# The output projection of a hybrid attention block in seven products of quarter matrices instead of eight

## The chip, the core and the metric

The kernel runs on one core of one Trainium2 chip. The metric is the time of one execution on the device in microseconds (us), the median of several runs. A core has five engines with a queue each: TensorE (PE, its weight loads shown as PEld) multiplies matrices into PSUM, VectorE (DVE) and ScalarE (ACT) work elementwise from PSUM or SBUF, GpSimd (POOL) works elementwise from SBUF, and SyncE (SP) issues the DMA transfers. Each queue is worked off in order.

## What is computed

One layer with two attention branches. Cut to what matters here, with 1024 tokens and 1024 channels:

```
merged = sigmoid(mg_a) * (y_a @ w_branch_a) + sigmoid(mg_b) * (y_b @ w_branch_b)
x = x + gate * (merged @ w_out)
```

The last line is the output projection: a product of two 1024x1024 matrices in f32, then a row of gate factors and the residual.

## The kernel before

Every f32 matrix is kept as two parts, a high one rounded to the format of the fast matrix product (fp32r) and a low one, the rest. A product takes three matmuls, high with high, high with low and low with high (mm3, line 129). A matmul has 128 rows of K, 128 tokens and up to 512 columns.

The kernel has three stretches: normalization and the input projections, the attention of 16 heads with other matrix products woven in, and the output. The change begins behind the attention, at about 834 us.

**The merge.** fillers() (lines 957 to 1061) is a generator that emits the products that only have to be done in time. Its last 32 units multiply the branch outputs by w_branch, 16 for branch A and then 16 for branch B (kind 0 and 1; per block c of 128 channels two halves of 512 tokens, sh 0 and 1). A unit has 12 matmuls into one PSUM bank. For branch A, VectorE turns the bank into mA[c] (line 1036). For branch B it does three operations of 512 columns per unit: the gated product (mg, line 1039), the sum with mA (line 1040) and, one unit later, the low part hT_lo (line 1046); ScalarE writes the high part hT_hi between them (line 1041). hT_hi and hT_lo hold merged with channels on the partitions: block k of 8, 1024 tokens. The next block of branch weights is loaded by SyncE (load_w, line 102) and split by ScalarE (line 115) and VectorE (line 116). The banks go round over five (fbanks = "fgott").

**The weights w_out.** w_out_load(0) is emitted when branch A's products are (line 1058): four loads of 512 KB, in slots of U, a pool of 29 pieces of SBUF of 4 KB per partition which are handed out oldest first; a load waits on SyncE's queue until its slot's last reader is done, and all later transfers wait behind it. In branch B's units with c from 2 to 5 one piece each is split, the high part on ScalarE, the low part on GpSimd (line 1060). w_out_load(1) stands ahead of output().

**The output.** output() (line 1345) goes through 16 units, 8 tiles of 128 tokens for the left 512 columns and then for the right:

```
for k in range(KT):
    wh, wl = self.wo[c][k // 2]
    self.mm3(acc, self.hT_hi[:, k, sl], self.hT_lo[:, k, sl], wh[:, k % 2, ls], wl[:, k % 2, ls],
             k == 0, k == KT - 1)
nc.vector.tensor_tensor(out=ot[:, ls], in0=acc, in1=gbc[:, cs], op=ALU.mult)
nc.vector.tensor_tensor(out=ot[:, ls], in0=ot[:, ls], in1=x[:, ls], op=ALU.add)
nc.sync.dma_start(t["out"][st * P:(st + 1) * P, cs], ot[:, ls])
```

That is 24 matmuls and two VectorE operations (lines 1375 and 1376) per unit, in the banks t, t, o and f in turn. The last unit is done in two halves of 256 columns. GpSimd and ScalarE split the right half of w_out during the units 2 to 5. x comes in pieces of 512 columns from Hs, a pool of 11 slots of 2 KB.

Of the kernel before, what the change touches and what calls it, by code (L numbers as in the profile page):

```python
# [41 lines left out]
class Slots:  # L42
    """Equal pieces of SBUF, taken and given back by hand; the one given back longest ago goes first."""
# [31 lines left out]
class Net:  # L75
# [7 lines left out]
    # ------------------------------------------------------------ helpers  # L83
    def rsqrt(self, ssq, n, count, tag, between=iter(())):
        """between: other work of the vector engine, for the time each step waits for the one before."""
        nc, pool = self.nc, self.sp
        v, y, a = (pool.tile([P, 32], F32, tag=f"rs_{q}", name=f"{q}_{tag}", bufs=2)[:, 0:n] for q in "vya")
        nc.vector.tensor_scalar(out=v, in0=ssq, scalar1=1.0 / count, scalar2=EPS, op0=ALU.mult, op1=ALU.add)
        nc.vector.tensor_scalar(out=y.bitcast(I32), in0=v.bitcast(I32), scalar1=-0.5, scalar2=float(0x5F3759DF),
                                op0=ALU.mult, op1=ALU.add)  # L90
        for _ in range(3):
            next(between, None)
            nc.vector.scalar_tensor_tensor(out=a, in0=y, scalar=-0.5, in1=y, op0=ALU.mult, op1=ALU.mult)
            next(between, None)
# [143 lines left out]
    # ------------------------------------------------------------ phase 0  # L238
    def phase0(self):
# [71 lines left out]
        def broadcast_c():  # L311
            """c along the free dimension of every partition, through a diagonal and a product with ones."""
# [15 lines left out]
        def ada_rows(kt, bank):  # L328
            """The shift of a block whose rows lie on the partitions."""
# [193 lines left out]
    # ------------------------------------------------------------ latents  # L523
# [211 lines left out]
    # ------------------------------------------------------------ branch A operands  # L735
# [190 lines left out]
    def gate_sum(self, chs, engine="d"):  # L926
        """128 columns of the adaLN gate each."""
# [15 lines left out]
    def gate_row(self):  # L943
        """The gate as a row, quartered (the two factors of a half that the merge gates leave out)."""
# [12 lines left out]
    def fillers(self):  # L957
        """All GEMMs that only have to be done in time, some matmuls at a time; True where an accumulation ends."""
# [29 lines left out]
        low, mA = [], {}  # L988
        yield from self.g1b(first)
        for pos, (k, u) in enumerate(todo):  # L990
# [40 lines left out]
            else:  # L1031
# [5 lines left out]
                else:  # L1037
                    mf = mA[c][:, sl]
                    nc.vector.scalar_tensor_tensor(out=m, in0=m, scalar=1.0, in1=acc, op0=ALU.add, op1=ALU.mult)
                    nc.vector.tensor_tensor(out=mf, in0=mf, in1=m, op=ALU.add)  # L1040
                    nc.scalar.copy(self.hT_hi[:, c, sl], mf)
                    low.append((c, sh))
                    while len(low) > (pos + 1 < len(todo)):
                        c1, s1 = low.pop(0)
                        x = (slice(None), c1, slice(s1 * 512, s1 * 512 + 512))
                        nc.vector.tensor_tensor(out=self.hT_lo[x], in0=mA[c1][:, x[2]], in1=self.hT_hi[x].bitcast(F32),  # L1046
                                                op=ALU.subtract)
                        if s1:
                            U.put(mA.pop(c1))
                Hs.put(m)  # L1050
            if last:
# [3 lines left out]
                if kind == 0 and c == 7:  # L1055
                    for kk in range(4):
                        U.put(*self.y[kk])
                    self.w_out_load(0)
            if kind == 1 and sh == 1 and c in (2, 3, 4, 5):
                self.w_out_split(0, c - 2)  # L1060
            yield 1300. if kind == "t" and c < 8 else 1000.

    def w_out_load(self, c):
        self.wo[c] = [self.load_w(self.t["w_out"][c, k], [P, 2, 512], f"wo{c}{k}") for k in range(4)]

    def w_out_split(self, c, k):
        self.wo[c][k] = self.split(self.wo[c][k], f"wo{c}{k}", engine=self.nc.gpsimd)
# [63 lines left out]
    def prep_b(self, n):  # L1131
        """The same for heads n and n + 1 of branch B, turned together: rows 0-63 of a transpose are head n's."""
# [16 lines left out]
        def group(nm, src, vec, g):  # L1149
# [41 lines left out]
    def scores(self, n, i):  # L1191
        """Scores of q tile i of head n and their maximum; the rest of the softmax is returned."""
# [35 lines left out]
    def turn(self, n, g, j):  # L1228
        """Transposes k block j of P for q tiles 4g..4g+3; the products with V are returned."""
# [114 lines left out]
    # ------------------------------------------------------------ all  # L1344
    def output(self):
        nc, t, Hs, U = self.nc, self.t, self.Hs, self.U
        gbc = U.get([P, D], F32, "gbc")
        nc.sync.dma_start(gbc, self.gate_d.broadcast_to([P, D]))
        xt = {}

        def load(u):
            c, st = divmod(u, ST)
            xt[u] = Hs.get([P, 512], F32, f"xo{u}")
            nc.sync.dma_start(xt[u], t["x"][st * P:(st + 1) * P, c * 512:(c + 1) * 512])

        for u in range(3):
            load(u)
        for u in range(2 * ST):
            c, st = divmod(u, ST)
            if u + 3 < 2 * ST:  # L1360
                load(u + 3)
            if c == 0 and 2 <= st < 6:
                self.w_out_split(1, st - 2)
            sl = slice(st * P, (st + 1) * P)
            ot = Hs.get([P, 512], F32, f"ot{u}")
            x, n = xt.pop(u), 2 if u == 2 * ST - 1 else 1    # the last one in halves, for what follows its products
            for e in range(n):
                ls = slice(e * 512 // n, (e + 1) * 512 // n)
                cs = slice(c * 512 + ls.start, c * 512 + ls.stop)
                acc = self.bank("ttof"[(u + e) % 4], f"out{u}{e}")[:, ls]  # L1370
                for k in range(KT):
                    wh, wl = self.wo[c][k // 2]
                    self.mm3(acc, self.hT_hi[:, k, sl], self.hT_lo[:, k, sl], wh[:, k % 2, ls], wl[:, k % 2, ls],
                             k == 0, k == KT - 1)
                nc.vector.tensor_tensor(out=ot[:, ls], in0=acc, in1=gbc[:, cs], op=ALU.mult)
                nc.vector.tensor_tensor(out=ot[:, ls], in0=ot[:, ls], in1=x[:, ls], op=ALU.add)
                nc.sync.dma_start(t["out"][st * P:(st + 1) * P, cs], ot[:, ls])
            Hs.put(ot, x)

    def build(self):  # L1380
# [28 lines left out]
        self.passes, self.qk, self.v, self.p, self.gates, self.y, self.wo = {}, {}, {}, {}, {}, {}, {}  # L1409
        self.extra = []  # L1410
# [5 lines left out]
        with tc.manual_schedule():  # L1416
# [40 lines left out]
            self.w_out_load(1)  # L1457
# [3 lines left out]
# ---------------------------------------------------------------- host layout  # L1461
# [72 lines left out]
```

## Time and profile before

| what | us |
|---|---|
| median of 3 runs | 991.84 |
| lowest and highest run | 989.53 and 992.6 |
| profiled execution: its span (no other time of it is given) | 989.3 |

| engine | busy us | share of the span |
|---|---|---|
| PE | 954.5 | 96% |
| DVE | 659.8 | 67% |
| ACT | 475.7 | 48% |
| POOL | 250.8 | 25% |

A span runs from the first to the last instruction of an execution. Busy time is an average over all stages; what a stage is limited by shows in the slices of the page, in the order of time, and in what ended each engine's waits. A row of the timeline with x2 or more is several instructions in a row, with the time from the start of the first to the end of the last. The VectorE instructions overlap a little: the next can start before the one ahead is written off, so the distance between starts counts for a sum, not the duration.

### The profile page before, as it was taken

What the parts mean: (1) busy time and instruction counts of PE and PEld (TensorE: products, weight loads), DVE (VectorE), ACT (ScalarE), POOL (GpSimd) and SP (SyncE); (2) the same over time, 40 slices, a digit from 0 to 9 for tenths busy, and PEclk for the clock granted to TensorE, in tenths of its full rate; (3) what the DMA queues carried; (4) which work ended last, traced back from release to release, by engine and by line L of the source; (5) the groups of instructions that cost most, each with busy time, mean ns of one, the idle gap of its engine ahead of it and who ended that gap; (6) DMA issues with size and microseconds to landing.
All of it is one profiled execution on the core that took longest, in us unless ns stands there. A gap on an engine that the chain in (4) does not pass through costs nothing.

```text
span 989.3 us, 15335 instructions
## 1 busy us (share of the span) xinstructions
PE 954.5 (96%) x5550; PEld 833.1 (84%) x5550; DVE 659.8 (67%) x1399; ACT 475.7 (48%) x962; POOL 250.8 (25%) x279
## 2 busy tenths in 40 slices
PE   6479999999999999999999999999999999999998
PEld 6379999999998888888888888888888888887887
DVE  6997787676734766757667667677676767495222
ACT  6347653344334655655646566566565644143000
POOL 4843222220001222221223233333332220045000
PEclk9889999999999999999999999999999999999999
DMA  9733113346485223424224232231321554643321
GB/s 345 285 128 131 52 55 107 124 150 221 155 251 149 67 95 84 139 66 109 84 65 119 77 108 66 86 109 65 118 87 45 181 181 148 228 148 126 100 92 64
DMA packets 80700, 123.95 MB, mean 125 GB/s; under 512 B 5896, under 2 KB 47504, under 8 KB 80624
## 3 DMA queue, kind: packets, MB, share of 16 engines
q1 hardware_dynamic: 80624, 122.96, 38.1%
q8 instruction: 44, 0.72, 0.3%
q14 instruction: 32, 0.26, 0.1%
HBM read 87.29 MB, written 35.66 MB: 124 GB/s over the span
## 4 chain that ended last, share of the span: by engine, by line
PE 85%; DVE 8%; DMA 4%; issue 1%; ACT 1%; SPq 0%; POOL 0%; ACTq 0%; DVEq 0%; POOLq 0%
PE f L127 31%; PE b L127 12%; PE out L127 9%; PE s L127 8%; PE o L127 7%; PE pt L136 6%; PE q L127 3%; PE ckv L127 2%; PE kv L127 2%; DVE hT_lo L1046 1%; DVE hT_lo L365 1%; DMA ks_u<-ka_d 1%; DVE wada_u L339 1%; PE cq_s L127 1%; DVE xT L359 1%
## 5 line engine op out<-in xcount | busy, mean ns | idle before, releaser
L1240 ACT CAST pp_u<-pt 128x512 fp32r<-128x512 f32 x192 | 92.1, 480 | 181.6 <-PE pt L136 167.8
L1241 DVE TENSOR_TENSOR pp_u<-pt,pp_u 128x512 fp32r<-128x512 f32 x192 | 106.6, 556 | 79.2 <-ACT pp_u L1240 77.1
L127 PE MATMUL f<-hT_hi,hi_f_u 128*128 128x512 f32 x384 | 153.6, 400 | 0.0
L127 PE MATMUL f<-hT_hi,lo_f_u 128*128 128x512 f32 x384 | 153.4, 400 | 0.0
L127 PE MATMUL f<-hT_lo,hi_f_u 128*128 128x512 f32 x384 | 153.2, 399 | 0.0
L127 PE MATMUL s<-k_u,q_u 96*128 96x512 f32 (+6 forms) x480 | 116.4, 361 | 0.7 <-ACT p_h L1220 0.7
L127 PE MATMUL b<-hi_b_u,hT_hi 128*128 128x256 f32 x384 | 109.6, 285 | 0.0
L127 PE MATMUL b<-hi_b_u,hT_lo 128*128 128x256 f32 x384 | 108.6, 283 | 0.0
L127 PE MATMUL b<-lo_b_u,hT_hi 128*128 128x256 f32 x384 | 108.6, 283 | 0.0
L1224 POOL TENSOR_SCALAR p_u<-p_u,rs 128x640 f32<-128x640 f32 (+1 forms) x64 | 65.2, 1018 | 164.4 <-DVE rs L1223 95.9
L1224 POOL TENSOR_SCALAR p_h<-p_h,rs 128x128 f32<-128x128 f32 (+1 forms) x64 | 38.6, 603 | 245.5 <-DVE rs L1223 205.7
L1214 DVE TENSOR_REDUCE nm<-s 128x1 f32<-128x128 f32 (+7 forms) x128 | 97.0, 758 | 4.4
L127 PE MATMUL o<-pp_u,v_u 128*128 128x512 f32 (+7 forms) x384 | 94.2, 340 | 0.0
L127 PEld LDWEIGHTS f<-hT_hi,lo_f_u 128*128 128x128 f32 x384 | 72.4, 189 | 11.9
L127 PEld LDWEIGHTS f<-hT_lo,hi_f_u 128*128 128x128 f32 x384 | 72.5, 189 | 11.2
L127 PEld LDWEIGHTS f<-hT_hi,hi_f_u 128*128 128x128 f32 x384 | 72.5, 189 | 11.1
L127 PEld LDWEIGHTS s<-k_u,q_u 96*128 96x128 f32 (+2 forms) x480 | 76.7, 190 | 6.1 <-ACT p_h L1220 1.2
L127 PEld LDWEIGHTS o<-pp_u,v_u 128*128 128x128 f32 (+1 forms) x384 | 61.8, 161 | 19.6
L127 PEld LDWEIGHTS b<-lo_b_u,hT_hi 128*128 128x128 f32 x384 | 73.6, 192 | 0.3
L127 PEld LDWEIGHTS b<-hi_b_u,hT_hi 128*128 128x128 f32 x384 | 73.6, 192 | 0.3
L127 PEld LDWEIGHTS b<-hi_b_u,hT_lo 128*128 128x128 f32 x384 | 73.6, 192 | 0.0
L136 PEld LDWEIGHTS pt<-ident,p_u 128*128 128x128 f32 x416 | 52.7, 140 | 16.6
(319 smaller groups left out, 2072.0 us busy)
## 6 DMA issues: line engine op xcount, KB each, us to landing
raw_f_u<-in_w_t SPq DMA_DIRECT2D x24, 512.0 KB
wada_u<-in_w_ada SPq DMA_DIRECT2D x16, 512.0 KB
mg_d<-th_h SPq DMA_DIRECT2D x32, 256.0 KB
mg_h<-mg_d SPq DMA_DIRECT2D x32, 256.0 KB
raw_b_u<-in_w_b SPq DMA_DIRECT2D x12, 512.0 KB
x_u<-in_x SPq DMA_DIRECT2D x8, 512.0 KB
raw_wg_u<-in_w_gate SPq DMA_DIRECT2D x8, 512.0 KB
va_d<-vhl_u SPq DMA_DIRECT2D x8, 512.0 KB
```

The costliest lines, as they stand in the source:

```text
L127: self.nc.tensor.matmul(out, lhsT=l, rhs=r, start=start, stop=stop)
L136: self.nc.tensor.transpose(out=out, in_=in_, identity=self.ident)
L339: nc.vector.scalar_tensor_tensor(out=w, in0=w, scalar=1.0, in1=self.cb, op0=ALU.mult, op1=ALU.mult, accum_out=a)
L359: (nc.vector if engine == "d" else nc.gpsimd).tensor_scalar(out=xT[:, kt, c], in0=xT[:, kt, c], scalar1=gs[:, kt, 1:2], scalar2=gs[:, kt, ...
L365: nc.vector.tensor_tensor(out=lo[:, kt, c], in0=xT[:, kt, c], in1=hi[:, kt, c].bitcast(F32), op=ALU.subtract)
L1046: nc.vector.tensor_tensor(out=self.hT_lo[x], in0=mA[c1][:, x[2]], in1=self.hT_hi[x].bitcast(F32), op=ALU.subtract)
L1214: nc.vector.tensor_reduce(out=nm, in_=sv, axis=AX.X, op=ALU.max, negate=True)
L1224: nc.gpsimd.tensor_scalar(out=p[:, 0:w], in0=p[:, 0:w], scalar1=rs, scalar2=0.0, op0=ALU.mult, op1=ALU.add)
L1240: nc.scalar.copy(ph[:, c0:], pt[:, c0:])
L1241: nc.vector.tensor_tensor(out=pl[:, c0:], in0=pt[:, c0:], in1=ph[:, c0:].bitcast(F32), op=ALU.subtract)
```

## The change

The matrices merged and w_out are cut in quarters: A11 and A12 are the left and right 512 channels of tokens 0 to 511, A21 and A22 those of tokens 512 to 1023; B11, B12, B21 and B22 are the quarters of w_out. Seven products of sums of quarters take the place of the eight products of quarters (named by their weights in the code):

```
11: A11 B11    21: A12 B21    T3: (A11-A21)(B22-B12)
S1 = A21+A22   S2 = S1-A11    S4 = A12-S2
T1 = B12-B11   T2 = B22-T1    T4 = B21-T2
T2: S2 T2      T1: S1 T1      T4: A22 T4      22: S4 B22
```

Each product is four token tiles of 4 k blocks, 12 matmuls a unit of 512 columns, into four banks: "nsg" (s is one double bank, taken as two halves) and "ttof" in turn. Sums of the merged quarters, of the weights and of the results are tensor_tensor operations on VectorE, in place where they can be. hT holds A11 and A12 for tokens 0 to 511, and for 512 to 1023 A11-A21 in the blocks 0 to 3 and A22 in 4 to 7; S2, S1 and S4 are later written over A11, A11-A21 and A12. Quarters of w_out are loaded again where they are needed a second time. Cut to its core:

```diff
 # fillers()
+                    if sh and c < 4:
+                        mf = Hs.get([P, 512], F32, f"dA{c}")
+                        nc.vector.tensor_tensor(out=mf, in0=mA[c][:, 0:512], in1=mA[c][:, 512:1024], op=ALU.subtract)
                     nc.scalar.copy(self.hT_hi[:, c, sl], mf)
...
-                    self.w_out_load(0)
-            if kind == 1 and sh == 1 and c in (2, 3, 4, 5):
-                self.w_out_split(0, c - 2)
+                    self.wo_load(0, 0)
+            if kind == 1 and sh == 1 and c in (1, 2):
+                self.wo_split("11", self.wr[0, 0], (c - 1,), self.nc.gpsimd)
+            if kind == 1 and sh == 1 and c == 2:
+                U.put(*self.wr.pop((0, 0)))
+                self.wo_load(1, 1)
+                self.wo_load(0, 1)
+            if kind == 1 and sh == 1 and c == 6:
+                self.wo_sum((1, 1), (0, 1), ALU.subtract)
+                U.put(*self.wr.pop((0, 1)))
...
+    def wo_load(self, r, c):
+        self.wr[r, c] = [self.load_w(self.t["w_out"][c, 2 * r + i], [P, 2, 512], f"wo{r}{c}{i}") for i in range(2)]
+    def wo_sum(self, dst, other, op, into=0):
+        for i in range(2):
+            a, b = self.wr[dst][i], self.wr[other][i]
+            self.nc.vector.tensor_tensor(out=(a, b)[into], in0=a, in1=b, op=op)
+    def wo_split(self, name, raws, parts=(0, 1), engine=None):
+        engine = engine or nc.gpsimd
+        for i in parts:
+            hi, lo = (self.U.get([P, 2, 512], F32R, f"w{e}{name}{i}") for e in "hl")
+            for k in range(2):
+                nc.scalar.copy(hi[:, k], raws[i][:, k])
+                engine.tensor_tensor(out=lo[:, k], in0=raws[i][:, k], in1=hi[:, k].bitcast(F32), op=ALU.subtract)
 # output()
+        def sum_a(dst, a, b, op):
+            for k in range(4):
+                nc.vector.tensor_tensor(out=dst(k), in0=a(k), in1=b(k), op=op)
+        def split_a(src, k0, cols):
+            for k in range(4):
+                nc.scalar.copy(hi[:, k0 + k, cols], src(k))
+            for k in range(4):
+                nc.vector.tensor_tensor(out=lo[:, k0 + k, cols], in0=src(k), in1=hi[:, k0 + k, cols].bitcast(F32),
+                                        op=ALU.subtract)
+        def product(acc, k0, tok, name, ls=slice(0, 512)):
+            for k in range(4):
+                wh, wl = self.wo[name][k // 2]
+                sl = slice(tok * P, (tok + 1) * P)
+                self.mm3(acc[:, ls], hi[:, k0 + k, sl], lo[:, k0 + k, sl], wh[:, k % 2, ls], wl[:, k % 2, ls],
+                         k == 0, k == 3)
+        def finish(u, acc, add=None, ls=slice(0, 512), ready=None):
+            if add is not None:
+                nc.vector.tensor_tensor(out=ot[:, ls], in0=src, in1=add[:, ls], op=ALU.add)
+                src = ot[:, ls]
+            nc.vector.tensor_tensor(out=ot[:, ls], in0=src, in1=gbc[:, cs], op=ALU.mult)
+            nc.vector.tensor_tensor(out=ot[:, ls], in0=ot[:, ls], in1=x[:, ls], op=ALU.add)
+            nc.sync.dma_start(t["out"][st * P:(st + 1) * P, cs], ot[:, ls])
...
+        self.wo_load(1, 0)
+        self.wo_load(0, 0)
+        self.wo_split("T3", self.wr[1, 1], engine=nc.vector)
+        X = banks("nsg")
+        self.wo_split("21", self.wr[1, 0])
+        for i in range(4):
+            product(X[i], 0, i, "11")
+            nc.scalar.copy(s1[i], X[i])
+            if i == 0:
+                self.wo_sum((1, 1), (0, 0), ALU.add)
+            if i == 1:
+                sum_a(s1f, s1f, lambda k: mA[4 + k][:, R], ALU.add)
+            if i == 2:
+                sum_a(s2f, s1f, s2f, ALU.subtract)
+        self.wo_split("T2", self.wr[1, 1])
+        split_a(s2f, 0, L)
+        Z = banks("ttof")
+        for i in range(4):
+            product(Z[i], 0, 4 + i, "T3")
+            nc.vector.tensor_tensor(out=a7[i], in0=Z[i], in1=s1[i], op=ALU.add)
+            if i == 0:
+                sum_a(s4f, s4f, s2f, ALU.subtract)
+        self.wo_load(0, 1)
+        self.wo_load(0, 0)
+        split_a(s1f, 0, R)
+        X = banks("nsg")
+        for i in range(4):
+            product(X[i], 4, i, "21")
+            if i == 1:
+                self.wo_sum((1, 0), (1, 1), ALU.subtract)
+                self.wo_load(1, 1)
+            if i == 2:
+                self.wo_sum((0, 1), (0, 0), ALU.subtract)
+                self.wo_split("T1", self.wr[0, 1])
+            finish(i, X[i], s1[i])
+        self.wo_split("T4", self.wr[1, 0])
+        split_a(s4f, 4, L)
+        Z = banks("ttof")
+        for i in range(4):
+            product(Z[i], 0, i, "T2")
+            nc.vector.tensor_tensor(out=s1[i], in0=Z[i], in1=s1[i], op=ALU.add)
+            nc.vector.tensor_tensor(out=e[i], in0=Z[i], in1=a7[i], op=ALU.add)
+        self.wo_split("22", self.wr[1, 1])
+        X = banks("nsg")
+        for i in range(4):
+            product(X[i], 0, 4 + i, "T1")
+            nc.vector.tensor_tensor(out=s1[i], in0=X[i], in1=s1[i], op=ALU.add)
+            finish(4 + i, X[i], e[i])
+        Z = banks("ttof")
+        for i in range(4):
+            product(Z[i], 4, 4 + i, "T4")
+            finish(8 + i, Z[i], e[i])
+        X = banks("nsg")
+        for i in range(4):
+            n = 2 if i == 3 else 1
+            for h in range(n):
+                ls = slice(h * 512 // n, (h + 1) * 512 // n)
+                product(X[i], 4, i, "22", ls=ls)
+                finish(12 + i, X[i], s1[i], ls)
```

mA[0..7] now keep their slots until the output is under way, and the order of the output is tokens 0 to 511 left, 512 to 1023 right, 512 to 1023 left, 0 to 511 right.

## Rows read from the trace of the kernel before

**Rows 1.** The page: TensorE and VectorE in 40 equal slices of the span.
```profile
PE   6479999999999999999999999999999999999998
DVE  6997787676734766757667667677676767495222
```

**Rows 2.** Chain of waits that ended last: start us, length us, what.
```profile
895.64 0.61 DVE mg_h L1039
896.29 89.29 PE out L127 x408
986.06 0.43 DVE ot_h L1376
```

**Rows 3.** VectorE, timeline in the merge: start us, us, line, operation, [idle<-releaser].
```profile
853.74 0.69 DVE L1039 SCALAR_TENSOR_TENSOR mg_h<-mg_h,f 128x512 f32<-128x512 f32 x1 [2.03 <-PE f L127]
...
859.57 1.29 DVE L116 TENSOR_TENSOR lo_f_u<-raw_f_u,hi_f_u 128x512 fp32r<-128x512 f32 x2 [4.42 <-ACT hi_f_u L115]
860.78 0.68 DVE L1039 SCALAR_TENSOR_TENSOR mg_h<-mg_h,f 128x512 f32<-128x512 f32 x1
861.50 0.69 DVE L1040 TENSOR_TENSOR mA_u<-mA_u,mg_h 128x512 f32<-128x512 f32 x1
862.11 0.69 DVE L1046 TENSOR_TENSOR hT_lo<-mA_u,hT_hi 128x512 fp32r<-128x512 f32 x1
862.71 0.68 DVE L1039 SCALAR_TENSOR_TENSOR mg_h<-mg_h,f 128x512 f32<-128x512 f32 x1
...
898.80 1.46 DVE L1046 TENSOR_TENSOR hT_lo<-mA_u,hT_hi 128x512 fp32r<-128x512 f32 x2
```

**Rows 4.** Waits between 834 and 990: us in total, times, longest.
```profile
PE out L127 <- DVE mg_h L1039: 1.8, 1, 1.8
```

**Rows 5.** VectorE, timeline in the output.
```profile
903.69 0.69 DVE L1375 TENSOR_TENSOR ot_h<-out,gbc_u 128x512 f32<-128x512 f32 x1 [3.43 <-PE out L127]
904.42 1.32 DVE L1376 TENSOR_TENSOR ot_h<-ot_h,xo_h 128x512 f32<-128x512 f32 x1
909.13 0.69 DVE L1375 TENSOR_TENSOR ot_h<-out,gbc_u 128x512 f32<-128x512 f32 x1 [3.40 <-PE out L127]
...
982.72 0.42 DVE L1375 TENSOR_TENSOR ot_h<-out,gbc_u 128x256 f32<-128x256 f32 x1 [1.46 <-PE out L127]
983.18 0.43 DVE L1376 TENSOR_TENSOR ot_h<-ot_h,xo_h 128x256 f32<-128x256 f32 x1
```

**Rows 6.** VectorE, timeline around GpSimd's first pair of weight splits.
```profile
873.65 1.78 DVE L1046 TENSOR_TENSOR hT_lo<-mA_u,hT_hi 128x512 fp32r<-128x512 f32 x1
875.35 0.68 DVE L1039 SCALAR_TENSOR_TENSOR mg_h<-mg_h,f 128x512 f32<-128x512 f32 x1
876.06 1.07 DVE L1040 TENSOR_TENSOR mA_u<-mA_u,mg_h 128x512 f32<-128x512 f32 x1
```

**Rows 7.** GpSimd, timeline: the first pair of weight splits, and eight in a row.
```profile
873.06 3.52 POOL L116 TENSOR_TENSOR lo_wo_u<-raw_wo_u,hi_wo_u 128x512 fp32r<-128x512 f32 x2 [54.59 <-DVE mg_h L1039]
...
900.13 10.50 POOL L116 TENSOR_TENSOR lo_wo_u<-raw_wo_u,hi_wo_u 128x512 fp32r<-128x512 f32 x8 [5.65 <-ACT hi_wo_u L115]
```

**Rows 8.** SyncE's queue, timeline around 850.
```profile
844.78 7.29 SPq L102 DMA_DIRECT2D raw_wo_u<-in_w_out  x4
852.12 0.42 SPq L102 DMA_DIRECT2D raw_f_u<-in_w_br  x1
```

**Rows 9.** Chain of waits, around 855: the load that VectorE waits for.
```profile
852.12 6.73 DMA raw_f_u<-in_w_br
```

**Rows 10.** VectorE, timeline early in the kernel: 1024 columns.
```profile
72.57 1.23 DVE L365 TENSOR_TENSOR hT_lo<-xT,hT_hi 128x1024 fp32r<-128x1024 f32 x1
73.71 1.10 DVE L116 TENSOR_TENSOR lo_cq_u<-raw_cq_u,hi_cq_u 128x424 fp32r<-128x424 f32 x2
```

**Rows 11.** VectorE, timeline: two operations with a PSUM source in a row.
```profile
838.33 1.28 DVE L1036 SCALAR_TENSOR_TENSOR mA_u<-mg_h,f 128x512 f32<-128x512 f32 x2
```

**Rows 12.** ScalarE, timeline: eight copies of 512 columns in a row.
```profile
899.45 4.26 ACT L115 CAST hi_wo_u<-raw_wo_u 128x512 fp32r<-128x512 f32 x8
```

More of the change, by code (lines that the diff above doesn't have):

```diff
@@ L986, in first @@
                 load(0)
-        low, mA = [], {}
+        low, mA = [], self.mA
         yield from self.g1b(first)
@@ L1040, in fillers @@
                     nc.vector.tensor_tensor(out=mf, in0=mf, in1=m, op=ALU.add)
+                    if sh and c < 4:
+                        mf = Hs.get([P, 512], F32, f"dA{c}")
+                        nc.vector.tensor_tensor(out=mf, in0=mA[c][:, 0:512], in1=mA[c][:, 512:1024], op=ALU.subtract)
                     nc.scalar.copy(self.hT_hi[:, c, sl], mf)
-                    low.append((c, sh))
+                    low.append((c, sh, mf))
                     while len(low) > (pos + 1 < len(todo)):
-                        c1, s1 = low.pop(0)
+                        c1, s1, m1 = low.pop(0)
                         x = (slice(None), c1, slice(s1 * 512, s1 * 512 + 512))
[L1046 to L1049, printed above, removed]
+                        nc.vector.tensor_tensor(out=self.hT_lo[x], in0=m1, in1=self.hT_hi[x].bitcast(F32), op=ALU.subtract)
+                        if s1 and c1 < 4:
+                            Hs.put(m1)
                 Hs.put(m)
@@ L1057, in fillers @@
                         U.put(*self.y[kk])
-                    self.w_out_load(0)
-            if kind == 1 and sh == 1 and c in (2, 3, 4, 5):
-                self.w_out_split(0, c - 2)
-            yield 1300. if kind == "t" and c < 8 else 1000.
[L1063 to L1067, printed above, removed]
+                    self.wo_load(0, 0)
[8 more added lines that the diff above has]
+                U.put(*self.wr.pop((0, 1)))
+            yield 1300. if kind == "t" and c < 8 else 1000.
+    def wo_load(self, r, c):
[5 more added lines that the diff above has]
+    def wo_split(self, name, raws, parts=(0, 1), engine=None):
+        nc = self.nc
+        engine = engine or nc.gpsimd
[4 more added lines that the diff above has]
+                engine.tensor_tensor(out=lo[:, k], in0=raws[i][:, k], in1=hi[:, k].bitcast(F32), op=ALU.subtract)
+            self.wo.setdefault(name, []).append((hi, lo))
     def load_y(self, br, k):
@@ L1346, in output @@
         nc, t, Hs, U = self.nc, self.t, self.Hs, self.U
+        mA, hi, lo = self.mA, self.hT_hi, self.hT_lo
         gbc = U.get([P, D], F32, "gbc")
         nc.sync.dma_start(gbc, self.gate_d.broadcast_to([P, D]))
+        L, R = slice(0, 512), slice(512, 1024)
         xt = {}
+        order = [(st, 0) for st in range(4)] + [(st, 1) for st in range(4, 8)] + [(st, 0) for st in range(4, 8)] + \
+            [(st, 1) for st in range(4)]
         def load(u):
-            c, st = divmod(u, ST)
@@ L1353, in load @@
-            xt[u] = Hs.get([P, 512], F32, f"xo{u}")
-            nc.sync.dma_start(xt[u], t["x"][st * P:(st + 1) * P, c * 512:(c + 1) * 512])
-        for u in range(3):
-            load(u)
[L1358 to L1378, printed above, removed]
@@ new lines, in load, with four @@
+            if u < 16:
+                st, c = order[u]
+                xt[u] = Hs.get([P, 512], F32, f"xo{u}")
+                nc.sync.dma_start(xt[u], t["x"][st * P:(st + 1) * P, c * 512:(c + 1) * 512])
+        def four(name):
+            pair = [U.get([P, 2, 512], F32, f"{name}{i}") for i in range(2)]
+            return pair, [pair[i // 2][:, i % 2] for i in range(4)]
+        def sum_a(dst, a, b, op):
+            for k in range(4):
+                nc.vector.tensor_tensor(out=dst(k), in0=a(k), in1=b(k), op=op)
@@ new lines, in split_a, with banks @@
+        def split_a(src, k0, cols):
[4 more added lines that the diff above has]
+                                        op=ALU.subtract)
+        s1f = lambda k: mA[k][:, R]
+        s2f = lambda k: mA[k][:, L]
+        s4f = lambda k: mA[4 + k][:, L]
+        def banks(tags):
+            out = []
+            for tag in tags:
+                b = self.bank(tag, f"out_{tag}{len(out)}")
+                out += [b[:, 0:512], b[:, 512:1024]] if tag == "s" else [b]
+            return out
@@ new lines, in product @@
+        def product(acc, k0, tok, name, ls=slice(0, 512)):
[5 more added lines that the diff above has]
+        def finish(u, acc, add=None, ls=slice(0, 512), ready=None):
+            st, c = order[u]
+            x = xt[u]
+            cs = slice(c * 512 + ls.start, c * 512 + ls.stop)
+            ot = Hs.get([P, 512], F32, f"ot{u}{ls.start}")
+            src = acc[:, ls]
+            if add is not None:
[4 more added lines that the diff above has]
+            nc.sync.dma_start(t["out"][st * P:(st + 1) * P, cs], ot[:, ls])
+            Hs.put(ot)
+            if ls.stop == 512:
+                Hs.put(xt.pop(u))
+                load(u + 4)
@@ new lines, in done @@
+        def done(name):
+            for pair in self.wo.pop(name):
+                U.put(*pair)
+        for u in range(4):
+            load(u)
+        self.wo_load(1, 0)
+        self.wo_load(0, 0)
+        self.wo_split("T3", self.wr[1, 1], engine=nc.vector)
+        X = banks("nsg")
+        s1s, s1 = four("p1_")
+        self.wo_split("21", self.wr[1, 0])
[4 more added lines that the diff above has]
+                self.wo_sum((1, 1), (0, 0), ALU.add)
+                U.put(*self.wr.pop((0, 0)))
+            if i == 1:
+                sum_a(s1f, s1f, lambda k: mA[4 + k][:, R], ALU.add)
+            if i == 2:
+                sum_a(s2f, s1f, s2f, ALU.subtract)
@@ new lines, in output @@
+        done("11")
+        self.wo_split("T2", self.wr[1, 1])
+        split_a(s2f, 0, L)
+        Z = banks("ttof")
+        a7s, a7 = four("a7_")
+        for i in range(4):
[3 more added lines that the diff above has]
+                sum_a(s4f, s4f, s2f, ALU.subtract)
+        done("T3")
+        self.wo_load(0, 1)
+        self.wo_load(0, 0)
+        split_a(s1f, 0, R)
+        for k in range(4):
+            U.put(mA.pop(k))
@@ new lines, in output @@
+        X = banks("nsg")
[3 more added lines that the diff above has]
+                self.wo_sum((1, 0), (1, 1), ALU.subtract)
+                U.put(*self.wr.pop((1, 1)))
+                self.wo_load(1, 1)
+            if i == 2:
+                self.wo_sum((0, 1), (0, 0), ALU.subtract)
+                U.put(*self.wr.pop((0, 0)))
+                self.wo_split("T1", self.wr[0, 1])
+                U.put(*self.wr.pop((0, 1)))
+            finish(i, X[i], s1[i])
@@ new lines, in output @@
+        done("21")
+        self.wo_split("T4", self.wr[1, 0])
+        split_a(s4f, 4, L)
+        for k in range(4, 8):
+            U.put(mA.pop(k))
+        Z = banks("ttof")
+        es, e = four("e_")
+        for i in range(4):
+            product(Z[i], 0, i, "T2")
+            nc.vector.tensor_tensor(out=s1[i], in0=Z[i], in1=s1[i], op=ALU.add)
+            nc.vector.tensor_tensor(out=e[i], in0=Z[i], in1=a7[i], op=ALU.add)
+        done("T2")
+        U.put(*self.wr.pop((1, 0)))
+        self.wo_split("22", self.wr[1, 1])
@@ L1409, in build @@
         self.passes, self.qk, self.v, self.p, self.gates, self.y, self.wo = {}, {}, {}, {}, {}, {}, {}
+        self.mA, self.wr = {}, {}
         self.extra = []
@@ L1456, in build @@
                 self.U.put(*self.y[kk])
-            self.w_out_load(1)
             self.output()
```

## The prediction

> **What bounds the kernel now.** I read the slices of the page first, then the chain of waits, then VectorE's timeline at the end, then GpSimd's and SyncE's. The slices show TensorE at nine tenths or more from the fourth slice on, and VectorE, once the start is over, at nine tenths only in slice 36; its last four are 5, 2, 2, 2 [rows 1]. One slice is 24.7 us, so the output has an idle VectorE and a full TensorE. The chain agrees: its last long piece is 89.3 us of output matmuls, with one VectorE operation behind it that starts at 986.06 and lasts 0.43 [rows 2]. But the chain reaches these matmuls through VectorE, not through TensorE: at the hand-over from merge to output TensorE waited 1.8 us for VectorE [rows 4], and the first output unit took 903.69 - 896.29 = 7.40 us where the next took 909.13 - 903.69 = 5.44 [rows 2, 5], 1.96 more, since VectorE still wrote low parts until 898.80 + 1.46 = 900.26 [rows 3]. That lag began when VectorE sat idle 4.4 us for a load of branch weights [rows 3], which took 6.73 us from its issue [rows 9]; SyncE had put four loads of w_out ahead of it, issued between 844.78 and 852.07 [rows 8].
>
> I count time t from the end of TensorE's merge work. Its first unit of branch B ended at 853.74 [rows 3]; a unit of 12 matmuls is half of 5.44, 2.72 us; 15 more end at 894.5. So the output's matmuls could have begun at t = 0 and began at t = 1.8; VectorE's last operation ended at 986.49, t = 92.0.
>
> **TensorE's side.** Before: 15 units of 24 matmuls, two halves of 2.87 us (the first ends at 982.72, 5.44 x 14 + 2.87 behind 903.69). After: 27 units of 2.72 and two halves of 1.43, together 76.3 us. The first product reads only blocks 0 to 3 of tokens 0 to 511, written long before, and the free banks n and s, so the 1.8 us and the 1.96 us go too. TensorE alone would end at t = 76.3 instead of 985.58 - 894.5 = 91.1, 14.8 us earlier; one more VectorE operation behind the last half costs 0.4. By TensorE alone the gain were 14.3 us.
>
> **VectorE's side.** The edits give VectorE nearly all that they take from TensorE. Distances between starts are the price. Two SBUF inputs of 512 columns: 0.61 (862.11 - 861.50) [rows 3]. 1024 columns: 73.71 - 72.57 = 1.14 [rows 10]. One PSUM source with an independent operation next: two in 1.28 us, so 0.60 each [rows 11]. An operation that reads the result of the one ahead starts 0.73 behind it (904.42 - 903.69) [rows 5]. In the output:
> 28 operations of 512 columns from SBUF (the T3 split, S1, S2, S4 and three splits, 4 each): 17.1;
> three sums of weights, 2 operations of 1024 each: 6.8;
> 16 with a PSUM source (4 behind T3, 8 behind T2, 4 behind T1): 9.6;
> 15 finishes of a chain of three, 0.73 + 0.73 + 0.61 = 2.07: 31.0;
> the last one in halves, 0.46 (983.18 - 982.72 [rows 5]) + 0.46 + 0.43 twice: 2.7.
> Sum 67.2 us, against 16 x 2 operations before.
>
> [...] My rows make PSUM and SBUF sources alike [rows 3, 11]. [...]
>
> *The hand-over.* Only two loads of w_out instead of four now stand ahead of the branch weights. I take half of the 6.73 us as gone [rows 9], so VectorE resumes at about 856.3 instead of 859.57, and its split is done at 857.5. From there: 15 units of 862.71 - 860.78 = 1.93 [rows 3], 29.0; four new subtractions for A11-A21, each reading what was just written, 0.73, 2.9; two more splits of branch weights at 1.21, 2.4; the new sum of weights 2 x 1.14, 2.3; the last low part 0.8; and four GpSimd operations in place of eight. A pair of those lengthens VectorE by 1.09 and 0.38 (1.78 and 1.07 for 0.69) [rows 6], 0.74 per GpSimd operation, 3.0. VectorE ends at 897.8, t = 3.3. Bounds: 2.6, where it is no later than TensorE's last unit, and 6.6, where the load comes no earlier. TensorE does not wait, since five banks go round.
>
> *GpSimd beside VectorE.* An operation of GpSimd and one of VectorE with two SBUF inputs do not overlap [rows 6, 7]: GpSimd's pair took 3.52 us, two pauses of 0.6 and two of 1.15 alone (eight in a row took 10.50, with two VectorE operations between); VectorE's operation from 873.65 took 1.78, one such 1.15 longer, while the one with a PSUM source beside it at 875.35 took its plain 0.68. They take turns. Now GpSimd splits five quarters behind the merge, 4 operations each. Walking the queues: the splits 21 and T2 fall on VectorE's sums and on S1 and S2, so 8 x 1.15 = 9.2; T1's fall on two finishes, whose first operation reads PSUM and goes past: 3.1; T4's fall on the low parts of S4, 4 x 1.15 = 4.6; 22's fall on the eight PSUM operations of product T2, nothing. Sum 16.9. Bounds: 12 of them at the 0.63 that the operation at 904.42 lost [rows 5], 7.6; all 20 at 1.16, 23.2. I take the walk, nearest to the rows of a busy VectorE.
>
> *The sum.* 3.3 + 67.2 + 16.9 = 87.4. In this walk VectorE never waits for TensorE: it starts 3.3 late, enters product 21 some 10 us behind, and ends 9 behind TensorE's last matmul. So the end is VectorE's: t = 87.4 against 92.0, **4.6 us less**, a span of 984.7 for 989.3. The page gives no time outside the span; the median of the runs is 2.5 above it, and 4.6 off 991.84 gives 987.2.
>
> **Waits checked.** T3's weights need four ScalarE copies at 0.53 [rows 12] and four subtractions behind t = 3.3: ready near 6, wanted at 10.9. 21's are ready near 14, wanted at 21.8. T2's and S2's near 25, wanted at 32.6. The quarters for T1 are loaded into slots that product T3 reads until t = 21.8; even with 6.73 us [rows 9] they land by 29 and VectorE asks for them at 39. T1's own split is the late one: its sum ends near 41, its last low part near 47, wanted from 43.5 on. TensorE stalls about 2 us there, which a 9 us slack swallows. SyncE's queue: the new loads stand ahead of the stores, and the second load of B11 waits for a slot that VectorE's sum frees, near 893, landing near t = 4, wanted near 6. The banks of one set are free 2 us before TensorE returns to them in product T2, the tightest place.
>
> **Rivals.** (a) *TensorE stays the bound.* GpSimd's operations cost VectorE about 0.63 each or less, and the sum falls to 3.3 + 67.2 + 7.6 = 78.1, where TensorE's 76.3 + 2 + 1.4 decide with 79.7: 12.3 less, 979.5. For it: VectorE idled 3.4 us in each output unit [rows 5]. Against it: the 1.78 us [rows 6]. Between it and the forecast lie 8 to 10 us of gain.
> (b) *Slower: the two halves of bank s count as one tile.* If a product into the second half has to wait until VectorE has read the first, then in products 21, T1 and 22 the third unit stands behind VectorE's finish of the second. Product 21 ends near 43 instead of 32.6, T1 near 69, T4 near 80, and in 22 the wait comes again: the last half ends near 92, VectorE at 93.4: 1.4 us slower than before, 993.2, and as much more as VectorE is late. It decides where that finish lies behind TensorE's own unit, from product 21 on. No row shows two halves of a bank in use by two engines.
> (c) *The hand-over stays late.* The load comes no earlier, or all 20 GpSimd operations cost their full 1.16: 6.6 or 23.2 in place of one term gives t = 90.7 or 93.7, 1.3 less to 1.7 more; 990.5 to 993.5.
>
> **How the numbers follow.** Forecast 0.53, rival (a) 0.17, (b) 0.12, (c) 0.18. The likeliest gives 987.2, its own range 984 to 991. A measurement of this kernel can tell about 0.3% from no change, 3 us. Faster by more: three quarters of the forecast, 0.40, and (a), together 0.57. Slower by more: the tails of (b) and (c) with further delay, 0.10. Within: 0.33. The range from 980.5 to 994.0 leaves out most of (a)'s far end and the tail where (b) or (c) meet more delay, some 2 in 10.
>
> **What would show it.** Right: no wait of TensorE at the hand-over; output matmuls of 76 to 79 us with one stall at T1's first unit; VectorE at nine tenths or more to the end, ending 7 to 11 us behind the last matmul; VectorE operations of 1.7 us beside GpSimd's in products 11 and T3. Wrong: VectorE waiting for TensorE in the last two products (then (a)), TensorE waiting before the third unit of a product in n, s, g (b), or VectorE's last low part of the merge beyond 900 (c). A stall that VectorE's queue spends on a DMA would overturn the walk.

## The result, and the profile after

The changed kernel takes 998.91 us, median of 14 runs, beside 989.96 us for 14 runs of the kernel before on the same chips: ratio 1.0084, 95% interval 1.0067 to 1.0100, **slower by 0.84%**. The forecast was 987.2 us, faster. The profiled run took 998.97 us.

The first thing to look at is the page, whose slices are now 24.9 us long.

```profile
span 997.2 us, 15352 instructions
...
PE 950.0 (95%) x5490; PEld 827.4 (83%) x5490; DVE 721.4 (72%) x1472; ACT 491.3 (49%) x990; POOL 264.7 (27%) x287
...
PE   6579999999999999999999999999999999998887
...
DVE  5997887686734666757657677667677766799986
...
PEclk9889999999999999999999999999999999999899
```

TensorE's last four slices, 9, 9, 9, 8 before [rows 1], are 8, 8, 8, 7, and VectorE's are 9, 9, 8, 6 for 5, 2, 2, 2. Neither engine is full to the end: two engines that take turns look like this. Who waits for whom is read from the waits of the kernel after, from 834 us to the end (engine, tile, line, releaser: us in total, times, longest). These are all the waits of TensorE for a reader of the output's banks, and the two longest of VectorE for TensorE there.

```profile
DVE ot_h L1428 <- PE out_s L127: 4.1, 3, 1.9
DVE p_u L1506 <- PE out_s L127: 3.2, 1, 3.2
PE out_g L127 <- DVE ot_h L1428: 1.1, 1, 1.1
PE out_s L127 <- ACT p_u L1452: 4.0, 1, 4.0
PE out_s L127 <- DVE ot_h L1428: 9.2, 3, 4.7
```

The wait of 1.8 us at the hand-over [rows 4] is gone, as forecast. In its place TensorE waits five times, 14.3 us in all, and each time for a reader of a bank of the set n, s, g (X in the code): four times of the double bank s, once of g. VectorE waits for TensorE in return. TensorE's timeline says where in a product that happens (start, duration, instruction, and in brackets the idle time ahead with its releaser). The rows are the first matmul of the output, of the unit that runs straight on into s, of each unit that waited, and of the units that follow the first two waits.

```profile
894.96 0.39 PE L127 MATMUL out_n<-wh_u,hT_hi 128*128 128x512 f32 x1
...
897.68 0.39 PE L127 MATMUL out_s<-wh_u,hT_hi 128*128 128x512 f32 x1
...
904.52 0.80 PE L127 MATMUL out_s<-wh_u,hT_hi 128*128 128x512 f32 x1 [3.95 <-ACT p_u L1452]
...
908.87 0.40 PE L127 MATMUL out_g<-wh_u,hT_hi 128*128 128x512 f32 x1
...
932.77 0.79 PE L127 MATMUL out_s<-wh_u,hT_hi 128*128 128x512 f32 x1 [4.69 <-DVE ot_h L1428]
...
938.06 0.59 PE L127 MATMUL out_g<-wh_u,hT_hi 128*128 128x512 f32 x1
...
961.24 0.50 PE L127 MATMUL out_s<-whT_u,hT_hi 128*128 128x512 f32 x1 [3.75 <-DVE ot_h L1428]
...
985.70 0.50 PE L127 MATMUL out_s<-wh_u,hT_hi 128*128 128x512 f32 x1 [0.79 <-DVE ot_h L1428]
...
991.32 0.39 PE L127 MATMUL out_g<-wh_u,hT_hi 128*128 128x256 f32 x1 [1.14 <-DVE ot_h L1428]
```

It is always the same place: the first unit into s runs straight on (897.68), the second unit into s, the third of its product, waits until the first unit into s has been read. That holds for products 11, 21, T1 and 22. The last wait is the second half of the last unit, which lies in the same bank g as the first half; before, the two halves had banks of their own.

The waits are not all of it. The unit behind the wait of 4.69 us took 938.06 - 932.77 = 5.29 us, the one behind the wait of 3.95 us took 908.87 - 904.52 = 4.35, where a unit takes 2.72 elsewhere. The windows of 5 us show the reason (us, then busy time and count of PE, PEld, DVE, ACT, POOL, then PEclk, DMA share, GB/s).

```profile
900.00:905.00 5.00, 1.05 (x4) 0.62 (x3) 5.00 (x6) 4.44 (x9) 3.06 (x2) 0.94 0.00 0
905.00:910.00 5.00, 5.00 (x17) 3.92 (x17) 5.00 (x3) 0.59 (x1) 4.61 (x3) 0.72 0.00 0
910.00:915.00 5.00, 5.00 (x23) 4.13 (x22) 4.88 (x7) 3.20 (x7) 1.96 (x2) 1.00 0.00 0
...
935.00:940.00 5.00, 5.00 (x16) 3.90 (x15) 3.11 (x4) 4.45 (x9) 3.90 (x3) 0.65 0.45 163
```

From 905 to 910 TensorE is busy all the time and gets through 17 matmuls where 23 fit into the next 5 us: the mean granted clock is 0.72, for 1.00 in the next 5 us; from 904.5 to 906 alone it is 0.50. TensorE had stood idle for 3.95 us ahead of it.

**The sum of it.** TensorE's output began at 894.96 and ended at 991.32 + 1.71 = 993.03, 98.1 us where the forecast had 76.3. By products, from one first matmul to the next: 11 took 16.6 us instead of 10.9, 21 took 18.5, T1 16.6, and 22 took 13.7 where its three units and two halves were to take 11.0. That is 5.8 + 7.6 + 5.7 + 2.7 = 21.8 us, all in the four products that use n, s and g; T3, T2 and T4 in the four single banks took their 10.9. Of it 14.3 are the waits above and some 6.5 the slower units behind them; the rest is the last matmul ahead of each wait, which runs out its 0.39 us where the next one otherwise starts 0.23 behind it.

### The profile page after: what moved, and what is told of

Its sections match the earlier page's. It is cut to its first block, busy times and chain, and to the rows that moved or that the text cites. A ratio compares the mean times of both kernels' runs of the same rounds, so it can differ in the third digit from the quotient of the medians.

```text
span 997.2 us, 15352 instructions
## 1 busy us (share of the span) xinstructions
PE 950.0 (95%) x5490; PEld 827.4 (83%) x5490; DVE 721.4 (72%) x1472; ACT 491.3 (49%) x990; POOL 264.7 (27%) x287
## 4 chain that ended last, share of the span: by engine, by line
PE 57%; DVE 8%; issue 2%; ACT 1%; DVEq 0%; ACTq 0%
PE f L127 31%; PE s L127 8%; PE o L127 7%; PE pt L136 6%; PE out_s L127 2%; DVE hT_lo L1400 1%; DVE hT_lo L1049 1%; DVE mg_h L1039 1%; PE out_g L127 1%; DVE mA_u L1040 1%; PE kt L136 1%; DVE ot_h L1428 1%; PE qt L136 1%; PE out_t L127 1%; DVE ot_h L1430 1%
## 5 line engine op out<-in xcount | busy, mean ns | idle before, releaser
L136 PEld LDWEIGHTS pt<-ident,p_u 128*128 128x128 f32 x416 | 52.7, 140 | 16.6
```

What stands on the lines that cost most here:

```text
L136: self.nc.tensor.transpose(out=out, in_=in_, identity=self.ident)
```

## The experiments

**1 and 2: the banks, from both sides.** Four banks that are four tiles in place of n, s, s, g:

```diff
-                b = self.bank(tag, f"out_{tag}{len(out)}")
-                out += [b[:, 0:512], b[:, 512:1024]] if tag == "s" else [b]
+                out += [self.bank(tag, f"out_{tag}{len(out)}")]
...
-        X = banks("nsg")
+        X = banks("wxyz")
...
+            self.ps2 = ctx.enter_context(tc.tile_pool(name="ps2c", bufs=1, space=PSUM))
```

> The changed kernel with four single banks in place of n, the two halves of s, and g; nothing else is different. Theory (the two halves of bank s count as one tile for the queue): TensorE's four waits before the third unit of a product (4.0, 4.7, 3.3 and 0.3 us in the changed kernel's profile) and the half-clock stretches behind them go, TensorE's output takes about 78 us, VectorE sets the end near 88 us after the merge's last matmul as in the prediction's walk, the span is 984 to 988 and the ratio to before 0.994 to 0.999. Rival (TensorE waits because VectorE and ScalarE are late with what the product reads, whatever the bank): the waits stay at other units, span 994 or more, ratio 1.004 or more.

Measured: 990.01 us beside 990.86, ratio 0.9992 (0.9980 to 1.0004): as fast as before, and 8.9 us less than the change as it is. The waits in the expected text are given as 3.3 and 0.3 us for T1 and 22; the rows above have 3.75 and 0.79. The waits went as the theory said, but the span, 989.0 us, lies just above its range of 984 to 988; where the difference went stands in the next part. The waits of TensorE in the output that are left, from the waits of this kernel:

```profile
PE out_z L127 <- DVE ot_h L1427: 8.0, 1, 8.0
...
PE out_w L127 <- POOL wlT_u L1089: 1.4, 2, 0.7
```

No third unit waits any more. The 1.4 us are the late split of T1, forecast at about 2. The 8.0 us stand ahead of the second half of the last unit, in the same bank and tile z as the first. VectorE's timeline of this kernel has its last operation of the merge, and its end:

```profile
900.10 1.46 DVE L1049 TENSOR_TENSOR hT_lo<-mA_u,hT_hi 128x512 fp32r<-128x512 f32 x2
...
984.82 0.42 DVE L1427 TENSOR_TENSOR ot_h<-out_z,p_u 128x256 f32<-128x256 f32 x1 [2.10 <-PE out_z L127]
...
985.74 0.42 DVE L1430 TENSOR_TENSOR ot_h<-ot_h,xo_h 128x256 f32<-128x256 f32 x1
```

From 901.56 to 986.16 are 84.6 us, with one wait of 2.1: the last half has to be computed after VectorE asks for it, and behind 8 idle us it took 2.94 us, at a granted clock of 0.50, where the half ahead of it took 1.59 (the clock of that stretch is in the last row here, from the windows of this kernel).

```profile
945.00:970.00 25.00, 25.00 (x112) 20.65 (x111) 24.62 (x33) 1.42 (x3) 11.63 (x8) 1.00 0.35 103
...
980.00:985.00 5.00, 2.93 (x12) 2.63 (x12) 2.76 (x7) 0.00 (x0) 0.00 (x0) 0.50 0.36 131
```

The other side: the kernel before, with its units put alternately into the two halves of one double bank.

```diff
+        sd = self.bank("s", "outs")
...
-                acc = self.bank("ttof"[(u + e) % 4], f"out{u}{e}")[:, ls]
+                acc = (sd[:, 0:512], sd[:, 512:1024])[(u + e) % 2][:, ls]
```

> The kernel before, but the output's units alternate between the two halves of the double bank s instead of t, t, o, f. Theory: each unit waits until VectorE has read the unit before, at least 0.75 us for each of 16 boundaries, more where the clock is granted lower behind the wait: 12 to 30 us longer than before, span 1001 to 1020. Rival (halves are told apart by address): a half is read 0.7 us after its unit and needed again 5.4 us later, so the span stays at 989 to 991.

Measured: 1005.4 us, one run. VectorE is far from full here (it waits 76.1 us for TensorE), and still every unit waits, 16 times and 12.4 us in all; from TensorE's timeline of this kernel:

```profile
901.26 0.50 PE L127 MATMUL outs<-hi_wo_u,hT_hi 128*128 128x512 f32 x1 [0.79 <-DVE ot_h L1376]
...
907.78 0.50 PE L127 MATMUL outs<-hi_wo_u,hT_hi 128*128 128x512 f32 x1 [0.78 <-DVE ot_h L1376]
```

A unit starts every 907.78 - 901.26 = 6.52 us, not 5.44: 0.78 of waiting for VectorE's read of the other half, one operation, 0.16 in which the last matmul ahead of the wait runs out, and 0.14 of slower matmuls behind it. The half that a unit writes to was read a whole unit earlier; what it waits for is the read of the other one, which has just been filled. So the coupling is a property of the double tile, not of a late VectorE; a late VectorE only makes the wait longer.

**3 to 5: is VectorE's side as priced?** In experiment 3, on top of 1, ScalarE copies in the place of GpSimd's twenty subtractions (the low parts of five weight quarters are left out):

```diff
-                engine.tensor_tensor(out=lo[:, k], in0=raws[i][:, k], in1=hi[:, k].bitcast(F32), op=ALU.subtract)
+                if engine is nc.vector or name == "11":
+                    engine.tensor_tensor(out=lo[:, k], in0=raws[i][:, k], in1=hi[:, k].bitcast(F32), op=ALU.subtract)
+                else:
+                    nc.scalar.copy(lo[:, k], raws[i][:, k])
```

> Four single banks as in e1, and the low parts of the weights of products 21, T2, T1, T4 and 22 are copies made by ScalarE, so that GpSimd does nothing in the output. What is left out: the subtraction in these low parts. Theory (GpSimd's operations hold VectorE's up, 16.9 us by the walk): VectorE falls from 88 to about 73 us and TensorE's 76 to 79 us decide: span 974 to 979. Rival (GpSimd costs VectorE little, VectorE's own work is the bound): within 3 us of e1.

Measured: 982.72 us, one run. VectorE's timeline of this kernel:

```profile
902.11 1.47 DVE L1049 TENSOR_TENSOR hT_lo<-mA_u,hT_hi 128x512 fp32r<-128x512 f32 x2
...
977.47 0.42 DVE L1433 TENSOR_TENSOR ot_h<-ot_h,xo_h 128x256 f32<-128x256 f32 x1
```

and its waits between 900 us and the end:

```profile
DVE hT_lo L1403 <- ACT hT_hi L1401: 6.6, 2, 3.8
...
DVE ot_h L1430 <- PE out_z L127: 0.9, 1, 0.9
```

977.89 - 903.58 = 74.3 us, of which 7.5 are waits, 6.6 of them for ScalarE, which now has twenty more copies. The span, 980.7, lies 1.7 above the theory's range. TensorE's first and last matmul of the output, and its only wait between them, show that this is not the output's doing:

```profile
898.31 0.39 PE L127 MATMUL out_w<-wh_u,hT_hi 128*128 128x512 f32 x1
...
974.83 0.39 PE L127 MATMUL out_z<-wh_u,hT_hi 128*128 128x256 f32 x1 [1.48 <-DVE ot_h L1430]
...
976.24 0.28 PE L127 MATMUL out_z<-wh_u,hT_lo 128*128 128x256 f32 x1
```

From 898.31 to 976.52 are 78.2 us, within the theory's 76 to 79; but the output began 3.8 us later than the 894.5 from which the theory counted. VectorE's waits for ScalarE fell in time that it had to spare: TensorE waited for VectorE once, 1.48 us, where the same wait is 1.14 in the change as it is. VectorE's own work is 74.3 - 7.5 = 66.8 us; the forecast's sum was 67.2. With GpSimd beside it (experiment 1) it was 84.6 - 2.1 = 82.5, so GpSimd's twenty operations cost VectorE 15.7 us, 0.79 each, where doing them itself would cost 0.61; forecast 16.9.

In experiment 4, also on top of 1, VectorE does the low parts of 21, T2, T1 and T4 itself; those of 22 stay with GpSimd.

```diff
-        self.wo_split("21", self.wr[1, 0])
+        self.wo_split("21", self.wr[1, 0], engine=nc.vector)
...
```

> Four single banks as in e1, and the low parts for products 21, T2, T1 and T4 are made by VectorE instead of GpSimd (22 stays on GpSimd). Theory: 16 operations more on VectorE cost 16 x 0.61 = 9.8 us and about 1 us of waiting for ScalarE's copies, the 16.9 us lost beside GpSimd go: 6 us less than e1, span 978 to 983, ratio 0.988 to 0.993. [...]

Measured: 986.81 us, ratio 0.9964 (0.9946 to 0.9983): faster than before, by less than expected (span 984.9 for 978 to 983). VectorE's timeline of this kernel shows what was left out of account:

```profile
939.45 4.68 DVE L1089 TENSOR_TENSOR wlT_u<-raw_wo_u,whT_u 128x512 fp32r<-128x512 f32 x4
944.06 3.58 DVE L1400 TENSOR_TENSOR hT_lo<-mA_u,hT_hi 128x512 fp32r<-128x512 f32 x4
```

Four such subtractions take 2.49 us elsewhere. GpSimd's four for 22, which in experiment 1 ran from 951.12 to 956.63 beside operations with a PSUM source, 0.67 or 0.68 us each, now begin at 938.95 and 945.47 and meet these: 2.2 + 1.1 = 3.3 us. The wait ahead of the last half is there too, 7.3 us.

Experiment 5 takes both away: 22 goes to VectorE as well, and the last unit is not divided.

```diff
-        self.wo_split("22", self.wr[1, 1])
+        self.wo_split("22", self.wr[1, 1], engine=nc.vector)
...
-            n = 2 if i == 3 else 1
+            n = 1
```

> As e4, with 22's low parts on VectorE too and the last unit undivided. Theory (VectorE alone sets the end, and a half in the bank that VectorE still reads costs a wait of TensorE): in e4 the last half began 3 us late and cost 2.7 us more than one chain of three would; 22's four GpSimd operations lengthened VectorE by 3.4 us where four of its own cost 2.4. So 3.7 us less than e4: ratio to before 0.990 to 0.995, span near 981. Rival (the tail is a matter of the last transfer's size): twice the bytes at the end eat the gain, ratio 0.996 as e4.

Measured: 983.75 us beside 990.68, **ratio 0.9926 (0.9908 to 0.9945)**, as the theory had it: this version beats both kernels. The two edits were made together, so what each gives alone is not shown. The windows of this kernel, from 905 to 970 us:

```profile
905.00:970.00 65.00, 65.00 (x288) 53.87 (x287) 64.25 (x99) 17.95 (x33) 0.00 (x0) 1.00 0.40 128
```

and VectorE's last operation, from its timeline:

```profile
979.22 0.69 DVE L1430 TENSOR_TENSOR ot_h<-ot_h,xo_h 128x512 f32<-128x512 f32 x1
```

TensorE is busy for 65 us on end at a granted clock of 1.00 and done at about 973; VectorE follows and ends at 979.9. Both engines are full: what the change was to look like. By the terms above VectorE needs 66.8 + 20 x 0.61 - 0.6 for the undivided last unit = 78.4 us; from 901.8 to 979.9 are 78.1.

**6 and 7: two half measures in the change as it is.** In experiment 6 the two halves of s are not neighbours in a product: n, s, g, s.

```diff
-            return out
+            return [out[0], out[1], out[3], out[2]] if len(tags) == 3 else out
```

> The changed kernel with the order n, first half of s, g, second half of s, so that a unit lies between the two halves. Theory (a product into one half waits for the reader of the other): the waits of 4.0, 4.7 and 3.3 us move from the third unit to the fourth, and each is shorter by up to one unit, 2.7 us: span 988 to 994. Rival (the third unit waits for what it reads): the waits stay at the third unit, span 996 to 999.

Measured: 992.84 us, one run: 6.1 us less than the change as it is, about two thirds of what experiment 1 gave back. The wait has moved to the fourth unit; from TensorE's timeline of this kernel:

```profile
906.28 0.50 PE L127 MATMUL out_s<-wh_u,hT_hi 128*128 128x512 f32 x1 [1.49 <-ACT p_u L1452]
...
934.56 0.80 PE L127 MATMUL out_s<-wh_u,hT_hi 128*128 128x512 f32 x1 [6.19 <-DVE ot_h L1428]
```

Product 11's wait fell from 3.95 to 1.49. T1's fell from 3.75 to 1.52, and 22's is gone but for the 1.14 between the two halves of the last unit. That of 21 grew from 4.69 to 6.19: TensorE came to it earlier, VectorE no earlier.

Experiment 7 leaves the double bank and gives VectorE the low parts of 21, T2, T1 and T4, as experiment 4 did.

> The changed kernel with the two halves of s as they are, and the low parts for 21, T2, T1 and T4 on VectorE. Theory (the waits are as long as VectorE is behind TensorE): VectorE gains 6 us by the end of product T2, so the waits in products 21 and T1 shrink by most of their 4.7 and 3.3 us with the half-clock stretches behind them, the one in product 11, which waits for ScalarE, stays: span 987 to 992. Rival (the waits do not depend on VectorE's lag): span 996 to 999.

Measured: 996.2 us, one run: 2.7 us less than the change as it is. The span, 994.4, lies between the range of the theory and that of the rival. From TensorE's timeline of this kernel, the third units of 11, 21 and T1:

```profile
905.21 0.80 PE L127 MATMUL out_s<-wh_u,hT_hi 128*128 128x512 f32 x1 [3.96 <-ACT p_u L1452]
...
931.49 0.50 PE L127 MATMUL out_s<-wh_u,hT_hi 128*128 128x512 f32 x1 [2.68 <-DVE ot_h L1428]
...
958.46 0.50 PE L127 MATMUL out_s<-whT_u,hT_hi 128*128 128x512 f32 x1 [3.27 <-DVE ot_h L1428]
```

The wait for ScalarE (3.96) stays, as expected. That of 21 shrank from 4.69 to 2.68, so the waits do depend on how late VectorE is. T1's is still 3.27, for 3.75, and VectorE's timeline ahead of T1 shows why:

```profile
941.59 4.67 DVE L1089 TENSOR_TENSOR wlT_u<-raw_wo_u,whT_u 128x512 fp32r<-128x512 f32 x4
946.19 3.58 DVE L1400 TENSOR_TENSOR hT_lo<-mA_u,hT_hi 128x512 fp32r<-128x512 f32 x4
```

As in experiment 4, GpSimd's four operations for 22 meet these subtractions, and VectorE loses 2.2 + 1.1 = 3.3 us, about as much as T1 then waits.

## Why the prediction was wrong

**The step that failed** is the one on the free banks, in "Waits checked": "The banks of one set are free 2 us before TensorE returns to them in product T2, the tightest place". It looked at the return to a set from the next product but one, and "TensorE's side" took n, s and g for four banks that are free one by one. The two halves of s are one tile, and in these runs a unit into one half stood until the other had been read: experiment 1 takes the double tile away and the waits go, experiment 2 puts one into the kernel before and they come. With that, TensorE's term of 76.3 us became 98.1, and the walk in which "VectorE never waits for TensorE" became one in which each waits for the other. The sign that was set for (b), TensorE waiting before the third unit of a product in n, s, g, is what the trace shows. Rival (b) had named this mechanism, its place in 21, T1 and 22, and the sign, at a chance of 0.12; its evidence was put as "no row shows two halves of a bank in use by two engines", which left open what experiment 2 settles.

**Rival (b)'s price was too small as well**, 1.4 us slower than before for 7.9 by the spans. By its own walk, counted from the end of the merge's matmuls (894.96 here), 21 was to end at 43, T1 at 69, T4 at 80 and VectorE at 93.4; they ended at 46.0, 73.5, 84.4 and 99.4. Three things were missing:
- Product 11. Its results are read by ScalarE, not by VectorE, so (b) passed it over. ScalarE's copy of the second unit stood behind eight weight casts; from ScalarE's timeline of the kernel after:

```profile
899.11 2.18 ACT L1088 CAST whT_u<-raw_wo_u 128x512 fp32r<-128x512 f32 x4
901.20 2.17 ACT L1088 CAST wh_u<-raw_wo_u 128x512 fp32r<-128x512 f32 x4
...
903.88 0.59 ACT L1452 COPY p_u<-out_s 128x512 f32<-128x512 f32 x1
```

  The unit was done at about 900.6, the copy began at 903.88: 5.8 us lost in this product, with the slower unit behind the wait.
- The slower matmuls behind a wait, some 6.5 us over the five waits.
- The two halves of the last unit in one bank. Before, they alternated; the sum priced them as if they still did.

The walk of VectorE shows the same from the other side: its end at 99.4 is 5.0 (end of the merge) + 82.5 (own work, as in experiment 1) + 10.6 of waits for TensorE (4.1 + 3.2 in the rows above, and five smaller ones of 3.3 together), and 1.3 that no row settles.

**What was right.** TensorE left the merge without a wait. The hand-over's load came earlier: the split of the branch weights now begins at 856.98 behind 1.21 us of idle time, where VectorE idled 4.42 [rows 3]:

```profile
856.98 1.29 DVE L116 TENSOR_TENSOR lo_f_u<-raw_f_u,hi_f_u 128x512 fp32r<-128x512 f32 x2 [1.21 <-ACT hi_f_u L115]
...
898.47 1.46 DVE L1049 TENSOR_TENSOR hT_lo<-mA_u,hT_hi 128x512 fp32r<-128x512 f32 x2
...
923.52 0.68 DVE L1467 TENSOR_TENSOR a_u<-out_t,p_u 128x512 f32<-128x512 f32 x1
924.12 0.68 DVE L1467 TENSOR_TENSOR a_u<-out_o,p_u 128x512 f32<-128x512 f32 x1
```

Its end, at 899.93, is 5.0 us behind TensorE's where 3.3 were forecast (bounds 2.6 to 6.6). VectorE's 67.2 measured 66.8 and GpSimd's 16.9 measured 15.7, so the sum of 84.1 was 82.5.

**PSUM sources.** Two operations that read PSUM start 924.12 - 923.52 = 0.60 apart, as much as those with two SBUF inputs (0.61 [rows 3]) and as the prediction's rows had it [rows 11], and VectorE's sum came out below the rows' value, 66.8 for 67.2, not above it.

**What the forecast would have been worth without the double bank.** Experiment 1 ended 986.16 - 896.57 = 89.6 us behind its merge, for 92.0 before: 2.4 of the 4.6 us. Of the rest 1.7 is the merge's later end and 2.1 the wait for the last half, less 1.6 of shorter work. Even these 2.4 us are not in the span, 989.0 for 989.3, since the merge's matmuls ended 2.1 us later in that trace than before (896.57 for 894.5). They ended later in all seven traces with the seven products, by 0.5 to 3.8 us, and 2.4 us of gain would be a ratio of 0.9976, just outside experiment 1's interval; so part of that shift may come with the change, but it is not shown. In experiment 2, whose code up to the output is that of before, they ended 0.35 us later too (894.85). The mean granted clock of the first 200 us, whose work the change leaves as it was, is 0.96 before, 0.95 after and 0.94 in experiment 1; whether that moves the merge's end no run shows, and what does stays open.

## What to carry to other kernels

Before two engines are to alternate between accumulators, count the tiles and not the banks: halves of one tile, s of 1024 columns as well as g or z of 512, were handed over as a whole wherever the output of a run here used them, with waits of up to 8.0 us, and the same work in four tiles was 8.9 us faster. A wait of TensorE is to be priced with the slower matmuls behind it, here some 6.5 us more for 14.3 us waited, over the five waits of the change. And where VectorE is full, splitting work off to GpSimd can cost it more than doing the work: 0.79 us an operation beside 0.61, which was a good part of the way to a version faster than both.

## What was not expected of the hardware

The matmuls behind TensorE's longer waits in the change (3.75, 3.95 and 4.69 us) started 0.43 us apart in stretches, at a granted clock of 0.50 (904.5 to 906, 934 to 938 and 963 to 964 us), and 0.23 apart at 1.00 (910 to 915 us). In the kernel before they did so too behind the wait of 1.79 us at the hand-over, from 897.70 to 900.69 (0.50 from 898 to 900 us), with no wait of TensorE in between: about 1.75 of the 1.96 us that the prediction put down to VectorE's low parts. Behind the waits of 0.78 us in experiment 2, too, the first matmuls were a little slower, 0.14 us in a unit. These waits thus cost more than their length.

In experiment 1 TensorE wrote single banks while VectorE read others: from 945 to 970 us TensorE was busy for 25.00 us and VectorE for 24.62, and the only wait of TensorE for VectorE in the output was the one of 8.0 us between the two halves in z. That the waits between halves come from the program's own semaphores is the author's reading; no run shows it: a double tile with its coupling taken away was not tried, nor two engines in one bank.
